# Feed-forward gate and up products by one level of Strassen's seven-product form

## The chip, the cores and the metric

The kernel runs on one core of one Trainium2 chip. The metric is the device time of one execution in microseconds (us), the median of three runs. Engines are named as in the profile: PE is TensorE (PEld its weight loads), DVE VectorE, ACT ScalarE, POOL GpSimd, SP SyncE, which issues most DMAs.

## The reference

One layer of a decoder on x of 512 x 1024: three token mixers, cross-attention, a SwiGLU feed-forward layer, each behind a residual and LayerNorm. What the change touches is the feed-forward layer, with D = 1024 and 2816 hidden features:

```
def swiglu(h, w_gu, w_down):
    gate, up = jnp.split(h @ w_gu, 2, axis=-1)
    return (jax.nn.silu(gate) * up) @ w_down
...
h = layer_norm(DN_ALPHA * h + swiglu(h, ffn_w_gu[l], ffn_w_down[l]), ln3_g[l], ln3_b[l])
```

## The kernel before

All of it stays in the core's memory except the weights, which stream in units of [128 x 1024] (512 KB). Matrix products run in fp32r, a reduced form, with operands split in two: a hi part (a copy into fp32r) and a lo part (the rest, again in fp32r). `mm3` makes three matmuls, hi by hi, hi by lo, lo by hi. For each weight unit ACT makes `whi` (copy of `raw`) and DVE `wlo` (`raw` minus `whi`). `take()` hands out a unit and at the same time issues the work for later ones: lo splits `AHEAD` = 3 units ahead, one hi split more, DMAs 3 further on; all these tiles come from one pool `wp` of 14 buffers of [128 x 1024].

The feed-forward layer has KF = 22 hidden tiles f of 128 features. `w_gu` holds two units for each f, gate then up; a unit is eight blocks of 128 input features (k) by 128 hidden features. `wstat` multiplies a unit by h2T, the transposed, split activations (eight k, 512 tokens, as two tiles c = 0, 1 of four k each): 24 matmuls of 512 columns into one PSUM bank, fg or fu. ACT makes Silu of fg (sl), DVE multiplies by fu, and sl is split again into act, the operand of the down projection `w_dn` (tiles p). The last eight splits wait until all f are done.

The first two f (four units) are special: h2T comes from the LayerNorm after cross-attention, tile by tile of 128 tokens (t = 0 to 3). For these units the first 256 columns (t = 0, 1) are multiplied before the tiles 2 and 3 are ready, and the second 256 columns behind them (PSUM tiles named f). A LayerNorm tile goes through ACT and DVE sums (lt, st), a power on POOL (st with mh), two DVE operations that make lh, and `ln_T`: per c four transposes into one PSUM bank (tp), an ACT copy h2Th and a DVE subtraction h2Tl, both from that bank.

Everything is recorded in the order in which the program is written: each engine runs its instructions in that order and waits for semaphores of the others. The generators of the LayerNorm tiles are run at `slot()` calls, by a cost model at build time. Every recorded operation stands on line 74 of before and line 75 of the changed kernel, so rows are told apart by their tile names.

Of the kernel before, what the change touches and what calls it, by code (L numbers as in the profile page):

```python
# [16 lines left out]
P = 128  # L17
# [140 lines left out]
def hybrid_kernel(ctx: ExitStack, tc: tile.TileContext, I, out, dbg=None):  # L158
# [25 lines left out]
    def W(s, dt):  # L184
        return wp.tile([P, 1024], dt, tag="w", name=nm(s))
# [52 lines left out]
    order += [("w_xv", i, 1024) for i in range(4, 8)]  # L238
    add("w_xq", 8)
    add("w_xo", 8)  # L240
    add("w_gu", 2 * KF)
    add("w_dn", KF)
    raws, splits = {}, {}
    st = {"dma": 0, "hi": 0, "split": 0}

    def dma_to(n):
        while st["dma"] < min(n, len(order)):
            i = st["dma"]
            name, j, size = order[i]
# [26 lines left out]
    def split_to(n):  # L276
        while st["split"] < min(n, len(order)):
            i = st["split"]
            hi_to(i + 1)
            st["split"] += 1  # L280
            if i < NK32:
                continue
            size = order[i][2]
            hi, lo, raw, whole = his.pop(i)
            if lo is None:
                low = W("wlo", F32R)
                lo = low[:, :size]
                splits[i] = (whole, low)
# [93 lines left out]

    def mm3(ps, w, x, first, last):
        T.matmul(ps, lhsT=w[0], rhs=x[0], start=first, stop=False)
        T.matmul(ps, lhsT=w[0], rhs=x[1], start=False, stop=False)
        T.matmul(ps, lhsT=w[1], rhs=x[0], start=False, stop=last)

    def cut(pair, *idx):
        return pair[0][idx], pair[1][idx]
# [967 lines left out]
    def proj_ln(name, actT, nk, hres, lnj, outT, final=False, need=None):  # L1357

        nu = nk // 2
        last = min(4, nu)

        def part(pss, un, w, ts, stop):
            for kk in range(2):
                k = 2 * un + kk
                for t in ts:
                    mm3(pss[t], cut(actT[k], ALL, slice(t * P, (t + 1) * P)),
                        cut(w, ALL, slice(kk * 512, kk * 512 + 512)), k == 0, stop and k == nk - 1)

        sts = [S("st", 7) for _ in range(NT)]

        def half(t, c, ps):
            V.scalar_tensor_tensor(hres[t][c], hres[t][c], ALPHA, ps, ALU.mult, ALU.add,
                                   accum_out=sts[t][:, c:c + 1])
            if c == 0:
                ln_first(hres[t][0], sts[t])

        first = [PS("p0") for _ in range(NT)]
        for un in range(nu):  # L1380
            w = take(name)
            if need is not None:
                need(un)
            part(first, un, w, range(NT), True)
            if un == 0:
                gb = ln_params(lnj)
            slot()
        second = [PS("p1") for _ in range(NT)]
        done = 0
        for un in range(nu - last):  # L1390
            w = take(name)
            part(second, un, w, range(NT), False)
            if done < NT:
                half(done, 0, first[done])
                done += 1
            slot()
        while done < NT:
            half(done, 0, first[done])
            done += 1
        ws = [take(name, min(AHEAD, NPAIR - 1 - un)) for un in range(last)]  # L1400
        hout, es = [None] * NT, []

        def tile_gen(t):
            h = ln_apply(hres[t], sts[t], gb)
# [6 lines left out]
            ln_T(h, t, outT)  # L1411
# [12 lines left out]
        return hout, es  # L1424
# [73 lines left out]
            slot()  # L1498
        eh.append(start_bg(head(h, qh)))

    def need_head(un):
        finish(eh[un])


    h2T8, h2T = new_T("h2T")
    h2, es = proj_ln("w_xo", oT, KD, h1, 2, h2T8, need=need_head)
    finish_all(es[0], es[1])
    pre = []
    for i in range(4):
        w = take("w_gu", min(AHEAD, NPAIR - 1 - i))  # L1510
        ps = PS("f0")
        wstat(ps, w, h2T, cols=slice(0, 256))
        pre.append((w, ps))
        slot()
    finish_all(*es)
    for i, (w, ps) in enumerate(pre):
        wstat(ps, w, h2T, cols=slice(256, 512))
        split_to(nxt[0] + AHEAD)
# [11 lines left out]

    act = [None] * KF
    late = []
    for f in range(KF):
        if pre:
            ps, ps2 = pre.pop(0), pre.pop(0)
        else:
            w = take("w_gu")
            ps = PS("fg")
            wstat(ps, w, h2T)
            ps2 = None  # L1540
        s = H("sl")
# [12 lines left out]
    del h2T
    for i, (f, s) in enumerate(late):
        if i % 4 == 0:
            l8 = (H8("act"), H8("act"))
        act[f] = (l8[0][:, i % 4], l8[1][:, i % 4])
        split(act[f][0], act[f][1], s)
# [95 lines left out]
```

## Time and profile before

| | |
|---|---|
| time, median of 3 runs | 1004.05 us (1003.15 to 1004.45) |
| profiled execution, its own time | 1004.38 us |
| its span, first to last instruction | 1002.7 us |
| PE busy | 985.8 us, 98% |
| DVE, ACT, POOL busy | 53%, 37%, 18% |
| mean granted clock of PE | 0.996 |

A busy share is an average over the whole span. What a stage waits for is read in that stage, from the chain that ended last and from the idle time ahead of single instructions. The granted clock is a share of 2.4 GHz.

### The profile page before, as it was taken

To read this page: it belongs to the slowest core of one execution; us is meant where nothing else is said; L and a number is where in the kernel's file an instruction comes from. 1 tells how busy PE (TensorE), PEld (TensorE's weight loads), DVE (VectorE), ACT (ScalarE), POOL (GpSimd) and SP (SyncE) were. 2 spreads that over 40 slices of the span, in tenths; PEclk is the share of its full clock that TensorE was granted. 3 is DMA by queue.
4 is the path that set the end of the run, shared out by engine and by line. 5 is a ranking of instruction groups with operands and counts; after the bars stand their busy time and mean duration, and the time that the engine had idled before them with its cause. 6 is when DMAs were issued, how large, how long until landed. Compare 5 with 4: busy or idle time off the path is not lost. (4 is left out here: it accounts for less than half of the span.)

```text
span 1002.7 us, 12403 instructions
## 1 busy us (share of the span) xinstructions
PE 985.8 (98%) x4856; PEld 816.1 (81%) x4856; DVE 532.8 (53%) x869; ACT 368.7 (37%) x598; POOL 185.3 (18%) x281
## 2 busy tenths in 40 slices
PE   9999999999999999999989999999999999999996
PEld 7788778877888888888878888988888888888885
DVE  5724897696586644465864547633423322342317
ACT  5644465523244225533354433332232222321301
POOL 1389960042515001020100000200000000000001
PEclk9999999999999999999999999999999999999999
DMA  9932223234343544354222311543342322222202
GB/s 348 346 128 88 83 99 116 86 104 128 105 137 129 166 148 143 135 199 165 89 102 83 105 64 42 180 167 111 126 131 84 105 106 84 106 105 106 84 21 85
DMA packets 38363, 123.75 MB, mean 123 GB/s; under 512 B 4864, under 2 KB 5280, under 8 KB 38304
## 3 DMA queue, kind: packets, MB, share of 16 engines
q1 hardware_dynamic: 29856, 97.79, 27.8%
q0 software_dynamic: 6592, 22.02, 6.7%
q10 hardware_dynamic: 1856, 3.15, 1.1%
q8 instruction: 38, 0.62, 0.2%
q14 instruction: 21, 0.17, 0.0%
HBM read 109.31 MB, written 11.53 MB: 121 GB/s over the span
## 5 line engine op out<-in xcount | busy, mean ns | idle before, releaser
L74 DVE TENSOR_TENSOR wlo<-raw,whi 128x1024 fp32r<-128x1024 f32 x162 | 196.8, 1233 | 84.8 <-PE p L74 52.1
L74 ACT ACTIVATE whi<-raw 128x1024 fp32r<-128x1024 f32 x162 | 169.4, 1057 | 99.0 <-PE p L74 45.0
L74 PE MATMUL p<-whi,act 128*128 128x512 f32 x352 | 108.4, 389 | 0.0
L74 DVE TENSOR_TENSOR sl<-sl,fu 128x512 f32<-128x512 f32 x20 | 13.8, 688 | 140.0 <-PE fu L74 92.5
L74 POOL TENSOR_TENSOR st<-st,mh 128x1 f32<-128x1 f32 x16 | 15.3, 957 | 393.7 <-DVE st L74 388.0
L74 PE MATMUL gt<-h0Th,whi 128*128 128x512 f32 x192 | 79.2, 413 | 0.0
L74 PEld LDWEIGHTS p<-whi,act 128*128 128x128 f32 x352 | 66.1, 188 | 13.7
L74 PE MATMUL gt<-h0Th,wlo 128*128 128x512 f32 x192 | 75.0, 391 | 0.0
L74 PE MATMUL gt<-h0Tl,whi 128*128 128x512 f32 x192 | 74.9, 390 | 0.0
L74 PE MATMUL p<-wlo,act 128*128 128x512 f32 x176 | 68.5, 389 | 0.0
L74 PE MATMUL fg<-h2Th,whi 128*128 128x512 f32 x160 | 62.3, 389 | 0.0
L74 PE MATMUL fg<-h2Tl,whi 128*128 128x512 f32 x160 | 62.3, 389 | 0.0
L74 PE MATMUL fg<-h2Th,wlo 128*128 128x512 f32 x160 | 62.2, 389 | 0.0
L74 PE MATMUL fu<-h2Th,whi 128*128 128x512 f32 x160 | 62.2, 389 | 0.0
L74 PE MATMUL fu<-h2Tl,whi 128*128 128x512 f32 x160 | 62.2, 389 | 0.0
L74 PE MATMUL fu<-h2Th,wlo 128*128 128x512 f32 x160 | 62.2, 389 | 0.0
L74 ACT ACTIVATE th<-gt,gbh 128x512 f32<-128x512 f32 x24 | 16.6, 692 | 99.2 <-PE gt L74 90.2
L74 ACT ACTIVATE sl<-fg 128x512 f32<-128x512 f32 x20 | 12.0, 598 | 97.7 <-PE fg L74 97.7
L74 PEld LDWEIGHTS gt<-h0Th,wlo 128*128 128x128 f32 x192 | 36.0, 188 | 7.7
L74 PEld LDWEIGHTS gt<-h0Th,whi 128*128 128x128 f32 x192 | 36.2, 189 | 5.8 <-issue 0.2
L74 PEld LDWEIGHTS gt<-h0Tl,whi 128*128 128x128 f32 x192 | 36.3, 189 | 5.6
L74 PE MATMUL p<-whi,oT 128*128 128x512 f32 x128 | 40.5, 391 | 0.0
(348 smaller groups left out, 2156.1 us busy)
## 6 DMA issues: line engine op xcount, KB each, us to landing
raw<-in_w_gu SPq DMA_DIRECT2D x44, 512.0 KB, 3.2
raw<-in_w_dn SPq DMA_DIRECT2D x22, 512.0 KB, 3.2
raw<-in_w_xk SPq DMA_DIRECT2D x8, 512.0 KB, 6.7
raw<-in_w_gatea SPq DMA_DIRECT2D x8, 512.0 KB, 3.2
raw<-in_w_gateb SPq DMA_DIRECT2D x8, 512.0 KB, 3.2
raw<-in_w_gatec SPq DMA_DIRECT2D x8, 512.0 KB, 3.8
raw<-in_w_xv SPq DMA_DIRECT2D x8, 512.0 KB, 3.6
raw<-in_w_mix SPq DMA_DIRECT2D x8, 512.0 KB, 3.5
```

The costliest lines, as they stand in the source:

```text
L74: return f(*a, **k)
```

## The change

The first four f stay in the plain form (two in halves, two whole). The other 18 are taken in 9 groups of two. In a group the weights of a pair of f and the activations are cut in two each: gate and up blocks by the two halves of k (b0: gate, lower half; b1: up, lower; b2: up, upper; b3: gate, upper, each [128 x 1024], loaded as two pieces of 256 KB), tokens in two halves of 256. Instead of eight products of half size there are seven, each of 24 matmuls of 256 columns, in the order 11, 12, s2, s1, s3, s4, 22 (p0 to p6 below), with the weights b0, b3, t2, t1, b2-b1, b2, t4. Here t1 = b1-b0, t2 = b2-t1, t4 = b3-t2. POOL makes these four differences, in the order t1, t2, b2-b1 (in place), t4. Sums of activations s1 to s4 are made on POOL too, once, from plain copies of the transposed tiles that ACT makes out of the tp banks; they are split like other operands.

The products 11, s2, s3 and 22 are summed in one PSUM bank, wb, s1 and s4 in wc, 12 is alone in wa. Partial sums are read out while the bank goes on being used: ACT copies wb after 11 (m1) and after s2 (u2), and wc after s1 (m5); DVE adds wa to m1, wb to m5 after s3, wc to u2 after s4. The results are sg = Silu(m1) * u2 and sh = Silu(wb) * m5. From the third group on one split of act is made per group; the others are made while `w_dn` runs, six k ahead (`need_act`). A DMA is now issued only when `room()` finds buffers for it.

```
+NPLAIN = 4
...
+        if n == 2:
+            load(1)
+            load(2)
+            b["t1"], b["t2"] = W("t1", F32), W("t2", F32)
+            G.tensor_tensor(b["t1"], b[1], b[0], ALU.subtract)
+            G.tensor_tensor(b["t2"], b[2], b["t1"], ALU.subtract)
+            del b[0]
+            return b["t2"]
+        if n == 3:
+            return b.pop("t1")
+        if n == 4:
+            G.tensor_tensor(b[1], b[2], b[1], ALU.subtract)
+            return b.pop(1)
+        if n == 5:
+            return b.pop(2)
+        t = W("t4", F32)
+        G.tensor_tensor(t, b[3], b["t2"], ALU.subtract)
...
-        dma_to(min(st["split"], i + 1 + AHEAD) + DMA_AHEAD)
+        prefetch(min(st["split"], i + 1 + AHEAD) + DMA_AHEAD)
...
+    def h2_T(h, t):
+        plain[t] = [H("hT0"), H("hT1")]
+        for c in range(2):
+            ps = PS("tp")
+            for i in range(4):
+                T.transpose(ps[:, i * P:(i + 1) * P], h[c][:, i * P:(i + 1) * P], ident)
+            dst = (ALL, ALL, slice(t * P, (t + 1) * P))
+            split(h2T8[0][c][dst], h2T8[1][c][dst], ps.rearrange("p (k t) -> p k t", t=P))
+            A.activation(plain[t][c], ps, AF.Copy)
+        if t < 2:
+            return
+
+        (a11, a12), (a21, a22) = plain[t - 2], plain[t]
+        G.tensor_tensor(a22, a21, a22, ALU.add)
+        G.tensor_tensor(a21, a11, a21, ALU.subtract)
+        G.tensor_tensor(a11, a22, a11, ALU.subtract)
+        G.tensor_tensor(a12, a12, a11, ALU.subtract)
+        sums[t] = {"s1": a22, "s2": a11, "s3": a21, "s4": a12}
...
+    def product(ps, w, n, first):
+
+        for e in range(2):
+            for k in range(4):
+                c = e * 512 + k * P
+                mm3(ps[:, 256 * e:256 * e + 256], cut(w, ALL, slice(c, c + P)), (pl[n, 0][k], pl[n, 1][k]),
+                    first and e == 0 and k == 0, k == 3, skip_group_check=True)
...
+    for d in range((KF - NPLAIN) // 2):
+        pa, pb, pc_ = PS("wa"), PS("wb"), PS("wc")
+        m1, m5, u2, sg, sh = H("m1"), H("m5"), H("u2"), H("sg"), H("sh")
+        step(pb, "11", True)
+        A.activation(m1, pb, AF.Copy)
+        step(pa, "12", True)
+        V.tensor_tensor(m1, pa, m1, ALU.add)
+        A.activation(sg, m1, AF.Silu)
...
+        step(pb, "s2")
+        A.activation(u2, pb, AF.Copy)
+        step(pc_, "s1", True)
+        A.activation(m5, pc_, AF.Copy)
+        step(pb, "s3")
+        V.tensor_tensor(m5, pb, m5, ALU.add)
+        step(pc_, "s4")
+        V.tensor_tensor(u2, pc_, u2, ALU.add)
+        V.tensor_tensor(sg, sg, u2, ALU.mult)
+        step(pb, "22")
+        A.activation(sh, pb, AF.Silu)
+        V.tensor_tensor(sh, sh, m5, ALU.mult)
...
+        if len(late) > 9:
+            act_split()
...
-    hout, es = proj_ln("w_dn", act, KF, hres, 3, None, final=True)
+    hout, es = proj_ln("w_dn", act, KF, hres, 3, None, final=True, need=need_act)
```

POOL's queue around the LayerNorm tiles and the first group. In before, behind the power of tile 2 (st, mh) stand the power of tile 3 and the DMAs that store h2:

```order
L74 TENSOR_TENSOR st_4975<-st_4975,mh 128x1
L74 TENSOR_TENSOR st_4976<-st_4976,mh 128x1
L74 TENSOR_TENSOR st_4977<-st_4977,mh 128x1
L74 DMA h2d<-lh_5284 128x512
L74 DMA h2d<-lh_5286 128x512
```

In the changed kernel the same place (hT are the plain copies):

```order
L75 TENSOR_TENSOR st_4976<-st_4976,mh 128x1
L75 TENSOR_TENSOR hT_5477<-hT_5476,hT_5477 128x512
L75 TENSOR_TENSOR hT_5476<-hT_5336,hT_5476 128x512
L75 TENSOR_TENSOR hT_5336<-hT_5477,hT_5336 128x512
L75 TENSOR_TENSOR hT_5337<-hT_5337,hT_5336 128x512
L75 TENSOR_TENSOR st_4977<-st_4977,mh 128x1
```

The four sums of tiles 0 and 2 have come in ahead of the power of tile 3.

ACT's queue in the middle of the hidden tiles. In before (sl reads fg, act is the hi part of a split):

```order
L74 ACTIVATE whi_6003<-raw_5936 128x1024
L74 ACTIVATE sl_6032<-fg_6007 128x512
L74 ACTIVATE whi_6036<-raw_5969 128x1024
L74 ACTIVATE act_6066<-sl_6032 128x512
L74 ACTIVATE whi_6072<-raw_6005 128x1024
```

In the changed kernel a group (t_6546 is t2, t_6545 t1, t_6681 t4 of the fourth group; raw_6539 is b2-b1; m is m1, then m5):

```order
L75 ACTIVATE whi_6549<-t_6546 128x1024
L75 ACTIVATE whi_6579<-t_6545 128x1024
L75 ACTIVATE sh_6381<-wb_6375 128x512
L75 ACTIVATE act_6607<-sl_5764 128x512
L75 ACTIVATE whi_6622<-raw_6539 128x1024
L75 ACTIVATE m_6614<-wb_6612 128x512
L75 ACTIVATE whi_6651<-raw_6542 128x1024
L75 ACTIVATE sg_6617<-m_6614 128x512
L75 ACTIVATE whi_6683<-t_6681 128x1024
L75 ACTIVATE u_6616<-wb_6612 128x512
L75 ACTIVATE whi_6715<-raw_6685 128x1024
L75 ACTIVATE m_6615<-wc_6613 128x512
```

Between two readings of wb (m, then u) now stand sg, which needs m with wa added by DVE, and the whi of t4, which needs POOL.

DVE's queue at the same place. In before:

```order
L74 TENSOR_TENSOR sl_5756<-sl_5756,fu_5764 128x512
L74 TENSOR_TENSOR act_5791<-sl_5756,act_5790 128x512
L74 TENSOR_TENSOR wlo_5794<-raw_5727,whi_5760 128x1024
L74 TENSOR_TENSOR wlo_5827<-raw_5729,whi_5796 128x1024
L74 TENSOR_TENSOR sl_5825<-sl_5825,fu_5833 128x512
```

In the changed kernel, the same group as above for ACT:

```order
L75 TENSOR_TENSOR wlo_6537<-raw_6480,whi_6510 128x1024
L75 TENSOR_TENSOR u_6379<-wc_6376,u_6379 128x512
L75 TENSOR_TENSOR sg_6380<-sg_6380,u_6379 128x512
L75 TENSOR_TENSOR wlo_6577<-t_6546,whi_6549 128x1024
L75 TENSOR_TENSOR sh_6381<-sh_6381,m_6378 128x512
L75 TENSOR_TENSOR act_6608<-sl_5764,act_6607 128x512
L75 TENSOR_TENSOR wlo_6619<-t_6545,whi_6579 128x1024
L75 TENSOR_TENSOR wlo_6649<-raw_6539,whi_6622 128x1024
L75 TENSOR_TENSOR m_6614<-wa_6611,m_6614 128x512
L75 TENSOR_TENSOR wlo_6679<-raw_6542,whi_6651 128x1024
L75 TENSOR_TENSOR wlo_6713<-t_6681,whi_6683 128x1024
```

The addition of wa to m (m1) stands behind the wlo of t2, t1 and b2-b1, where before a multiplication came after two wlo.

## Rows read from the trace of the kernel before

**Rows 1.** The page: the span, and busy us (share) xinstructions of each engine.

```profile
span 1002.7 us, 12403 instructions
...
PE 985.8 (98%) x4856; PEld 816.1 (81%) x4856; DVE 532.8 (53%) x869; ACT 368.7 (37%) x598; POOL 185.3 (18%) x281
```

**Rows 2.** The chain that ended last: start us, us, engine, tile, xinstructions.

```profile
634.88 8.63 PE f L74 x72
643.51 0.45 PE tp L74 x4
...
645.36 11.66 PE f L74 x95
...
662.48 5.44 PE fu L74 x24
...
874.64 119.69 PE p L74 x528
```

**Rows 3.** Stretches: from:to us, busy of each engine, PEclk, DMA share, GB/s.

```profile
512.00:516.00 4.00, 3.19 (x9) 2.55 (x10) 4.00 (x8) 1.11 (x2) 0.00 (x0) 0.71 0.11 45
516.00:520.00 4.00, 4.00 (x16) 3.21 (x15) 0.89 (x1) 0.03 (x1) 0.00 (x0) 0.86 0.00 0
...
644.00:648.00 4.00, 3.41 (x27) 2.97 (x26) 1.29 (x2) 1.07 (x2) 0.00 (x0) 1.00 0.93 363
...
656.00:874.00 218.00, 218.00 (x967) 180.66 (x966) 68.26 (x73) 61.25 (x78) 4.92 (x9) 1.00 0.32 110
```

**Rows 4.** Timeline of POOL with DVE idle: start us, us, operation, sizes.

```profile
86.40 0.46 POOL L74 TENSOR_TENSOR pw<-pw 128x128 f32<-128x128 f32 x1
...
253.03 1.08 POOL L74 TENSOR_TENSOR phr<-pq,pq 128x512 f32<-128x512 f32 x1
...
255.21 1.28 POOL L74 TENSOR_TENSOR phr<-phr,pht 128x512 f32<-128x512 f32 x1
256.45 1.07 POOL L74 TENSOR_TENSOR phi<-pq,pq 128x512 f32<-128x512 f32 x1
```

**Rows 5.** Groups by form: xcount | busy us, mean ns | idle before, releasers.

```profile
L74 DVE TENSOR_TENSOR wlo<-raw,whi 128x1024 fp32r<-128x1024 f32 x162 | 196.8, 1233 | 84.8 <-PE p L74 52.1 <-ACT whi L74 26.1 <-issue 2.9
L74 DVE TENSOR_TENSOR sl<-sl,fu 128x512 f32<-128x512 f32 x20 | 13.8, 688 | 140.0 <-PE fu L74 92.5 <-issue 39.6 <-ACT act L74 7.9
...
L74 ACT ACTIVATE whi<-raw 128x1024 fp32r<-128x1024 f32 x162 | 169.4, 1057 | 99.0 <-PE p L74 45.0 <-DVE wlo L74 15.1 <-issue 12.5
L74 ACT ACTIVATE sl<-fg 128x512 f32<-128x512 f32 x20 | 12.0, 598 | 97.7 <-PE fg L74 97.7
```

**Rows 6.** Timeline of DVE and POOL, 130 to 134 us.

```profile
130.09 1.51 POOL L74 TENSOR_TENSOR pht<-pq,pq 128x512 f32<-128x512 f32 x1
130.60 2.09 DVE L74 TENSOR_TENSOR wlo<-raw,whi 128x1024 fp32r<-128x1024 f32 x1
131.68 2.16 POOL L74 TENSOR_TENSOR phr<-phr,pht 128x512 f32<-128x512 f32 x1
```

**Rows 7.** Timeline of DVE and POOL at 317 us; br is a PSUM tile.

```profile
317.18 1.29 POOL L74 TENSOR_TENSOR phr<-phr,pht 128x512 f32<-128x512 f32 x1
...
317.56 0.69 DVE L74 SCALAR_TENSOR_TENSOR th<-th,br 128x512 f32<-128x512 f32 x1 [3.53 <-PE br L74]
```

**Rows 8.** DMA issues: xcount, KB each, median us from issue to landing.

```profile
raw<-in_w_gu SPq DMA_DIRECT2D x44, 512.0 KB, 3.2
...
res<-h2d POOLq DMA_DIRECT2D x8, 256.0 KB, 3.0
```

**Rows 9.** Timeline of ACT, POOL and DVE in the LayerNorm tiles, 634 to 641 us.

```profile
634.48 1.08 ACT L74 ACTIVATE h2Th<-tp 128x512 fp32r<-128x512 f32 x2 [0.94 <-PE tp L74]
...
638.23 0.99 POOL L74 TENSOR_TENSOR st<-st,mh 128x1 f32<-128x1 f32 x1 [10.49 <-DVE st L74]
...
639.25 1.42 DVE L74 SCALAR_TENSOR_TENSOR lh<-lt,st,lnp 128x512 f32<-128x512 f32 x2 [0.44 <-POOL st L74]
```

**Rows 10.** Timeline of PE at 512 us, with the idle time before.

```profile
512.81 0.50 PE L74 MATMUL xq<-h1Tl,whi 128*128 128x512 f32 x1 [2.77 <-DVE h1Tl L74]
```

More of the change, by code (lines that the diff above doesn't have):

```diff
@@ L240, in hybrid_kernel @@
     add("w_xo", 8)
-    add("w_gu", 2 * KF)
+    add("w_gu", 2 * NPLAIN)
+    for d in range((KF - NPLAIN) // 2):
+        for n in range(7):
+            order.append(("w_gu", (NPLAIN + 2 * d, n), 1024))
     add("w_dn", KF)
     raws, splits = {}, {}
+    blk = {}
     st = {"dma": 0, "hi": 0, "split": 0}
@@ L285, in split_to @@
             if lo is None:
-                low = W("wlo", F32R)
-                lo = low[:, :size]
-                splits[i] = (whole, low)
+                lo = W("wlo", F32R)[:, :size]
+                splits[i] = (whole, lo)
             else:
@@ L293, in hybrid_kernel, with room, prefetch @@
     nxt = [0]
+    keep = [0]
+    def room():
+        names = {x.name for b in blk.values() for x in b.values()} | {x.name for x in raws.values()}
+        names |= {x[2].name for x in his.values()}
+        return 2 * max(keep[0], 1) + 2 * len(splits) + len(his) + len(names) + 2 <= NBUF_W
+    def prefetch(n):
+        while st["dma"] < min(n, len(order)) and (not keep[0] and type(order[st["dma"]][1]) is int or room()):
+            dma_to(st["dma"] + 1)
     def take(name, ahead=AHEAD):
@@ L380, in finish_all, with mm3 @@
                     rush[0] = False
[L383 to L386, printed above, removed]
+    def mm3(ps, w, x, first, last, **k):
+        T.matmul(ps, lhsT=w[0], rhs=x[0], start=first, stop=False, **k)
+        T.matmul(ps, lhsT=w[0], rhs=x[1], start=False, stop=False, **k)
+        T.matmul(ps, lhsT=w[1], rhs=x[0], start=False, stop=last, **k)
     def cut(pair, *idx):
@@ L1410, in tile_gen @@
             yield T, h[0], h[1]
-            ln_T(h, t, outT)
+            if callable(outT):
+                outT(h, t)
+            else:
+                ln_T(h, t, outT)
             yield 0
@@ L1499, in hybrid_kernel, with need_head @@
         eh.append(start_bg(head(h, qh)))
-    def need_head(un):
-        finish(eh[un])
+    def need_head(k):
+        finish(eh[k // 2])
     h2T8, h2T = new_T("h2T")
-    h2, es = proj_ln("w_xo", oT, KD, h1, 2, h2T8, need=need_head)
+    pl, wr = {}, {}
+    for n, c, half in (("11", 0, 0), ("12", 1, 0), ("21", 0, 1), ("22", 1, 1)):
+        for part in range(2):
+            wr[n, part] = [h2T8[part][c][:, :, 256 * half:256 * half + 256]]
+            pl[n, part] = [h2T8[part][c][:, k, 256 * half:256 * half + 256] for k in range(4)]
@@ new lines, in place, with to_block @@
+    def place(n, part, *tiles):
+        m = 4 // len(tiles)
+        pl[n, part] = [tiles[j // m][:, (j % m) * 256:(j % m) * 256 + 256] for j in range(4)]
+        wr[n, part] = [x[:, 0:256 * m].rearrange("p (k t) -> p k t", t=256) for x in tiles]
+    def to_block(n, t, src):
+        ts = slice((t % 2) * P, (t % 2) * P + P)
+        src = src.rearrange("p (k t) -> p k t", t=P)
+        hi, lo = wr[n, 0], wr[n, 1]
+        m = max(len(hi), len(lo))
+        for i in range(m):
+            ks = slice(4 // m * i, 4 // m * (i + 1))
+            at = [x[i][:, :, ts] if len(x) == m else x[0][:, ks, ts] for x in (hi, lo)]
+            split(at[0], at[1], src[:, ks])
@@ new lines, in hybrid_kernel @@
+    plain, sums = {}, {}
+    def h2_T(h, t):
[15 more added lines that the diff above has]
+        sums[t] = {"s1": a22, "s2": a11, "s3": a21, "s4": a12}
@@ L1515, in hybrid_kernel @@
     finish_all(*es)
-    for i, (w, ps) in enumerate(pre):
-        wstat(ps, w, h2T, cols=slice(256, 512))
-        split_to(nxt[0] + AHEAD)
+    del h1T, kx, vx, oT, h1
+    place("s1", 0, big.tile([P, 1032], F32R, tag="gx", name=nm("s1"), bufs=1))
+    place("s1", 1, big.tile([P, 1024], F32R, tag="tz", name=nm("s1")))
+    place("s2", 0, big.tile([P, 1024], F32R, tag="tz", name=nm("s2")))
+    place("s2", 1, H("s2", F32R), H("s2", F32R))
+    for part in range(2):
+        place("s4", part, H("s4", F32R), H("s4", F32R))
+    for i, (w, ps) in enumerate(pre):
+        half_plain(ps, w, 1)
+        if i < 3:
+            for t in (2, 3):
+                n = ("s2", "s1", "s4")[i]
+                to_block(n, t, sums[t][n])
+        keep[0] -= 1
+        split_to(nxt[0] + min(AHEAD, i + 1))
+        prefetch(st["split"] + DMA_AHEAD)
     pre = [ps for w, ps in pre]
@@ L1554, in hybrid_kernel, with act_tiles, act_split @@
[L1554 to L1559, printed above, removed]
+    l8 = []
+    def act_tiles(fs, t2s, s):
+        late.append((fs, t2s, s))
+    def act_split():
+        fs, t2s, s = late.pop(0)
+        n = len(t2s)
+        if len(late) < 8:
+            if not l8 or l8[0][2] == 4:
+                l8[:] = [[H8("act"), H8("act"), 0]]
+            hi, lo = l8[0][0][:, l8[0][2]], l8[0][1][:, l8[0][2]]
+            l8[0][2] += 1
+        else:
+            hi, lo = H("act", F32R), H("act", F32R)
+        split(hi, lo, s)
+        for i, f in enumerate(fs):
+            act[f] = act[f] or [None] * NT
+            for j, t in enumerate(t2s):
+                o = slice((i * n + j) * P, (i * n + j + 1) * P)
+                act[f][t] = (hi[:, o], lo[:, o])
@@ new lines, in hybrid_kernel, with place_s3 @@
+    for f in range(NPLAIN):
+        s = H("sl")
+        for i in range(2):
+            if f > 1:
+                w = take("w_gu")
+                pre.append(PS("fg" if i == 0 else "fu"))
+                wstat(pre[-1], w, h2T)
+                slot()
+            if i == 0:
+                A.activation(s, pre[0], AF.Silu)
+        V.tensor_tensor(s, s, pre[1], ALU.mult)
+        del pre[:2]
+        act_tiles([f], range(NT), s)
+    def place_s3():
+        for part in range(2):
+            pl["s3", part], wr["s3", part] = pl["21", part], wr["21", part]
+        for t in (2, 3):
+            to_block("s3", t, sums[t]["s3"])
+        sums.clear()
+        plain.clear()
@@ new lines, in product, with step @@
+    def product(ps, w, n, first):
+        for e in range(2):
+            for k in range(4):
+                c = e * 512 + k * P
+                mm3(ps[:, 256 * e:256 * e + 256], cut(w, ALL, slice(c, c + P)), (pl[n, 0][k], pl[n, 1][k]),
+                    first and e == 0 and k == 0, k == 3, skip_group_check=True)
+    def step(ps, n, first=False):
+        product(ps, take("w_gu"), n, first)
+        slot()
+    for d in range((KF - NPLAIN) // 2):
+        pa, pb, pc_ = PS("wa"), PS("wb"), PS("wc")
[5 more added lines that the diff above has]
+        A.activation(sg, m1, AF.Silu)
+        if d == 0:
+            place_s3()
+        step(pb, "s2")
[10 more added lines that the diff above has]
+        V.tensor_tensor(sh, sh, m5, ALU.mult)
+        fs = [NPLAIN + 2 * d, NPLAIN + 2 * d + 1]
+        act_tiles(fs, (0, 1), sg)
+        act_tiles(fs, (2, 3), sh)
+        if len(late) > 9:
+            act_split()
+        del m1, m5, u2, sg, sh, pa, pb, pc_
@@ L1560, in hybrid_kernel, with need_act @@
+    pl.clear()
+    wr.clear()
+    def need_act(k):
+        while late and (act[min(k + 6, KF - 1)] is None or None in act[min(k + 6, KF - 1)]):
+            act_split()
     hres = load_res(h2d)
-    hout, es = proj_ln("w_dn", act, KF, hres, 3, None, final=True)
+    hout, es = proj_ln("w_dn", act, KF, hres, 3, None, final=True, need=need_act)
     finish_all(*es)
```

52 lines of the change are left out of this document (27 added, 25 removed).

## The prediction

> **What bounds the kernel now.** I read the page first: the span is 1002.7 us and TensorE (PE) is busy for 985.8 of it, the other engines for about half or less [rows 1]. Then the chain that ended last: behind the LayerNorm tiles it is nothing but PE, 24 matmuls per weight unit of the feed-forward layer, and then the down projection p without a break [rows 2]. The table by stretches says the same: from 656 to 874 us PE is busy 218.00 of 218.00 us at granted clock 1.00, VectorE (DVE) 68, ScalarE (ACT) 61, GpSimd (POOL) 5 [rows 3]. So less PE time shortens the kernel directly, and every wait that the change puts before a matmul lengthens it directly; there is no slack to hide one in.
>
> **Term 1, the products.** A 512-column matmul takes 119.69 us / 528 = 226.7 ns in p, and 5.44 / 24 = 226.7 in fu; a 256-column one, with its own weight load as here, 8.63 / 72 = 119.9 ns [rows 2]. Half the columns cost 0.53, not 0.5. Eighteen of 22 f leave the plain form: 36 units x 24 = 864 matmuls x 226.7 = 195.8 us. In their place come 9 groups x 7 products x 24 = 1512 matmuls x 119.9 = 181.3 us. Term 1 is **-14.5 us**; a group of two f goes from 21.8 to 20.15 us, a product is 2.88.
>
> **Term 2, GpSimd's sums, and what they hold up.** Each group needs t1, t2, b2-b1 and t4, subtractions of 128x1024 in SBUF, which no row shows. With two dense inputs 128x512 takes 1.28 us and 128x128 0.46 [rows 4]: 2.14 ns an element, so 1024 take about 2.38; as starts stand 0.04 before the end ahead of them, I take G = 2.3. Bounds: twice the 1.08 of the same size with operands that repeat, less one fixed part of 0.18, is 1.98; twice 1.28 is 2.57. The dense row is nearest.
>
> The Trainium skill, "GPSIMD Engine Reference", section 3.1, gives 4497 ns for a two-input addition of 2048 elements; half of it, 2.25, is an estimate by that page. By it the sum below comes out 1.4 us lower. The row stays.
>
> DVE and POOL don't run side by side here. At 130.09 a POOL operation is running; the wlo that DVE starts at 130.60 lasts 2.09 us, against 1.23 on the average [rows 5, 6], and the POOL operation behind it, 131.68, lasts 2.16, against 1.28. Each waits for the other to end. A DVE operation with one input in PSUM was not held: 0.69 us in the middle of a POOL one [rows 7]. So I treat each operation of two SBUF inputs as exclusive; m1, m5 and u2, added from PSUM, are not.
>
> The Trainium skill, "SBUF — State Buffer", section "Who interferes with whom", speaks against this change: a DVE instruction with two SBUF inputs and a GpSimd one that reads SBUF share one pair of ports, and the later waits for the whole of the earlier. By that rule the waits below must come, without it term 2 would be nil; the rows at 130 us agree with it.
>
> Now one group, in us from the start of its fifth product (p4, s3), in the order in which the engines are fed. Durations: wlo 1.15 and whi 1.0 in a row, a 512 operation 0.65 on DVE and 0.6 on ACT [rows 5].
> - The loads of the next group's b1 and b2 get buffers when p3 ends and land about 3.2 later [rows 8], SP having two more to issue: t1 can start at 3.5. It runs to 5.8; a wlo that waits meanwhile follows to 6.95; t2 to 9.25.
> - b2-b1 and the DVE multiplication sg*u2 share the next 2.3 + 0.65, whichever is first: 12.2. wlo of t2 to 13.35, sh*m5 and the lo of act to 14.65.
> - t4 needs the buffer of b3, free when the next group's second product (p1) ends at 14.4. It and the wlo of t1 take 3.45, again in either order: 18.1. wlo of b2-b1 to 19.25.
> - Only now does DVE come to m1 += wa, which could have run at 14.6: it ends at 19.9. ACT has Silu (sg) next and behind it, in its fixed order, the whi of t4 and then the copy u2 = wb: 20.5, 21.5, 22.1.
> - p4 of the next group writes over the bank that this copy reads. It was due at 20.15 and starts at 22.1: about 1.9 us a group. Some of that falls on p3, if t4 goes ahead of the wlo of t1; the sum is the same.
>
> The chain holds four POOL operations, so p4 starts at 12.9 + 4G: on time for G below 1.8. The first groups begin with idle queues; I charge seven of the nine: **+13.3 us**. Bounds of G: 0.7 a group (+4.7) and 3.0 (+21). Landings 0.5 later add 3.5. [...]
>
> **Term 3, the LayerNorm tiles.** Before, ACT has h2Th of tile t=2 done at 635.5, POOL the power of tile 3 at 638.23 to 639.2 and DVE its lh at 640.7, well ahead of PE, which transposes it at 643.51 when the first halves of four units are done [rows 2, 9]. Each plain copy added on ACT comes behind h2Tl of DVE, which reads the same bank and itself stands behind lh and wlo; ACT then makes its three whi later. For t=1 the two copies cost PE about 0.35 us (h2Th of c=1 comes after the first copy). For t=2 the copies and the later whi put the end of its second copy at about 639.8. POOL then makes the four sums of tiles 0 and 2 (4 x 1.28 = 5.1, and 0.7 for DVE between), and only behind them the power of t=3, its place in POOL's queue: 645.6 to 646.6. With the first lh 0.75 later (two take 1.42 [rows 9]) the transposes start at 647.4, where PE, 0.35 late, was ready at 643.9: 3.5 us idle. A last 0.5 is the copy between the two h2Th of t=3. Together 4.4.
>
> So long a pause lowers the clock. After 2.77 us of idle PE the granted clock was 0.71 and 0.86 in the next two stretches of 4 us [rows 3, 10], 1.2 GHz for part of them: (0.29 + 0.14) x 4 = 1.7 us lost. Term 3 is **+6.1 us**, from 2 (copies not in the way, sums ended within the slack of 2.8) to 9 (DVE's chain of small operations held by each sum as well).
>
> **At nothing.** Further loads: twice as many pieces of half the size, 256 KB landing in 3.0 us, 512 KB in 3.2 [rows 8]; SP only issues. The splits of s1, s2, s3, s4 lie under the second halves of four units, 11.66 us [rows 2], and under the plain f of 21.8, on engines that are a third busy; if they came late, the third product would wait for them, once. The splits of act that w_dn now asks for as it goes lie under p of 2.7 us a k, against 1.3 for one split. In the down projection nothing else changes.
>
> **Sum.** -14.5 + 13.3 + 6.1 = +4.9 us: span 1007.6. Outside the span lie 1.7 us (the profiled execution has 1004.38), which makes 1009.3; the profiled execution stands 0.3 above the median of the runs, so the median should be **1009.0**. What a measurement can tell from no change is 0.2%, 2.0 us: faster is below 1002.0, slower above 1006.1.
>
> **Rivals.** First, faster: the sums fit under the products. One mechanism decides, the length of a POOL subtraction. At G = 2.1 the wait is 1.2 a group, 8.4 in seven, and the gain and both losses cancel; at 1.98 the time is 1000.4; and if POOL and DVE were not exclusive for these operands, term 2 is nil and the time 994 to 996. For it: the 1.08 row, and that POOL is otherwise idle. Against: both operands are dense, and rows 6. Chance 0.28.
>
> Second, longer waits: G = 2.57, or landings of 3.7, since loads now wait for buffers that only POOL frees: 1013 to 1020. For it: the 2.16 row, and that POOL is never the one that goes first in my chain. Against: loads land in 3.2 with DMA a third busy. Chance 0.17.
>
> Third, the change doesn't do what it says: a 256-column matmul in a group runs longer than 119.9, because the weight loads show 816.1 us of busy time [rows 1] and there are as many as matmuls. 10% more would be 18 us: 1027. Against it stands the row of 72 such matmuls with as many loads. Chance 0.03.
>
> **How the numbers follow.** The forecast has 0.52, its own range is 1005 to 1014 (G from 2.15 to 2.45, term 3 from 4 to 8). Of the 0.28 of the first rival 0.04 lies above 1002.0, and that part and 0.08 of the forecast's lower end are within 0.2%: same 0.12. Faster holds the other 0.24 of the first rival, and 0.02 from a forecast whose term 3 vanishes: 0.26. Slower is the rest, 0.42 + 0.17 + 0.03 = 0.62. The range that leaves out 0.1 on each side reaches into both rivals: 997 to 1018.
>
> **What would show it.** In the trace after: matmuls of the products 120 ns apart; POOL's 128x1024 subtractions 2.2 to 2.4 us where alone, 3 and more where DVE is ahead; wlo up to 3.4; PE idle before the first matmul of s3 by ACT's u2 (or before s1 by DVE's wlo of t1), 1.5 to 2.3 us from the third group on; the period of a group 21.5 to 22.5; PE idle before tp of t=3 by 3 to 5 us, with the clock below 1.00 behind it. If the groups come every 20.2 us, term 2 was wrong; if tp comes at 644, term 3.

## The result, and the profile after

The changed kernel takes **1019.94 us** (median of 4 runs, 1018.62 to 1021.16) beside 1004.25 for the kernel before (median of 4 in the same runs): ratio 1.0154, 95% interval 1.0134 to 1.0175. It is slower, as forecast, but by 15.7 us where 4.9 were forecast, and it lies 1.9 us above the range (997 to 1018).

The page, for [rows 1] and [rows 8]:

```profile
span 1019.5 us, 14088 instructions
...
PE 981.0 (96%) x5504; PEld 840.3 (82%) x5504; DVE 633.9 (62%) x935; ACT 417.1 (41%) x672; POOL 288.9 (28%) x325
...
raw<-in_w_gu SPq DMA_DIRECT2D x72, 256.0 KB, 3.9
```

PE does less work (981.0 us for 985.8), and the span is 16.8 longer. The chain that ended last, for [rows 2]:

```profile
652.94 12.71 PE f L75 x95
665.65 5.47 PE fg L75 x24
...
687.43 2.87 PE wb L75 x24
690.31 2.88 PE wa L75 x24
...
891.59 114.28 PE p L75 x504
```

The stages are cut in the timeline of PE, at the first matmul of f, of fg, of what the groups replace (of the groups themselves in the changed kernel) and of p. Before:

```profile
630.23 0.28 PE L74 MATMUL f<-h2Th,whi 128*128 128x256 f32 x1
656.85 0.40 PE L74 MATMUL fg<-h2Th,whi 128*128 128x512 f32 x1
678.64 0.39 PE L74 MATMUL fg<-h2Th,whi 128*128 128x512 f32 x1
874.48 0.39 PE L74 MATMUL p<-whi,act 128*128 128x512 f32 x1
```

and after:

```profile
631.59 0.28 PE L75 MATMUL f<-h2Th,whi 128*128 128x256 f32 x1
665.48 0.40 PE L75 MATMUL fg<-h2Th,whi 128*128 128x512 f32 x1
687.27 0.28 PE L75 MATMUL wb<-h2Th,whi 128*128 128x256 f32 x1
891.43 0.40 PE L75 MATMUL p<-whi,act 128*128 128x512 f32 x1
```

This cuts the difference in three. The first matmul of f comes 1.4 us later. That isn't due to the change: its first new operation, ACT's plain copy of tile 0, stands at 624.81 us, and 1.3 of the 1.4 are there at 599.92 already (598.61 before). Behind the pause at 512 us the granted clock was 0.50 and 0.65 in the two stretches of [rows 3], for 0.71 and 0.86 before. In the runs below this matmul stands anywhere from 629.81 (e1) to 632.20 (e12). From it to the first fg PE needs 33.9 us, before 26.6: **+7.3**. The nine groups take 204.2 us, for 195.8 of the plain form: **+8.3**, where -1.2 was forecast. From p to the end it is 128.1 us, for 128.2. The products run at the forecast pace (2.88 us for 24), so the groups hold some 24 us beyond what they need without a wait (180.3 us, e1 below). The timeline of PE, for a group, the last group and tile 3 of the LayerNorm (in brackets idle us and what ended it):

```profile
650.44 1.94 PE L75 MATMUL tp<-ident,lh 128*128 128x128 f32 x8 [4.11 <-DVE lh L75]
...
786.39 0.38 PE L75 MATMUL wb<-h2Th,whi 128*128 128x256 f32 x1 [0.98 <-ACT u L75]
802.01 0.50 PE L75 MATMUL wb<-s,whi 128*128 128x256 f32 x2 [0.96 <-ACT m L75]
805.53 0.39 PE L75 MATMUL wc<-s,wlo 128*128 128x256 f32 x1 [0.18 <-DVE wlo L75]
809.36 0.38 PE L75 MATMUL wb<-h2Th,whi 128*128 128x256 f32 x1 [0.93 <-ACT u L75]
...
877.31 0.38 PE L75 MATMUL wb<-h2Th,whi 128*128 128x256 f32 x1 [0.99 <-ACT u L75]
884.13 0.80 PE L75 MATMUL wc<-s,whi 128*128 128x256 f32 x2 [3.69 <-ACT m L75]
```

The waits are largely where the forecast has them: 0.9 to 1.1 us before s3 by the copy u2, in eight groups, and 0.2 before s1 by DVE's wlo in six. Those before s2, 0.3 to 1.0 us by the copy m1, it doesn't name. From the first s3 that waits, 719.78, to the last, 877.31, seven groups take 22.50 us each. The last group has a pause of its own, 3.69 us before s4, by the copy m5, which nothing in the forecast pays for. The chain through one group says why 22.50:

```profile
807.21 1.14 DVE wlo L75
...
808.75 0.43 SPq L75
...
810.94 4.85 DMA raw<-in_w_gu
...
817.11 2.73 POOL t L75
...
819.87 1.07 ACT whi L75
...
820.96 1.47 DVE wlo L75
...
823.20 0.68 DVE sh L75
...
824.41 4.56 DVE wlo L75 x2
828.97 0.60 DVE m L75
829.57 1.14 DVE wlo L75
```

It begins and ends with the same instruction, the wlo of b2, 22.36 us apart, and PE isn't in it. The wlo of b2-b1 frees the buffer for the next group's b0, for which SP has waited 14.5 us (806.64), and the wlo of b2 the one for b3, 0.8 us more; the loads of b1 and b2 stand behind these in SP's queue, so that all eight pieces go out from 806.64 to 810.94. They land, POOL makes t1 and t2, ACT and DVE split t2, DVE is held by t4 (two wlo in 4.56 us), adds wa to m1, and only then comes to the next wlo of b2. What POOL and DVE do there, from the timeline:

```profile
814.62 2.40 POOL L75 TENSOR_TENSOR t<-raw,raw 128x1024 f32<-128x1024 f32 x1 [10.83 <-DVE wlo L75]
817.11 2.73 POOL L75 TENSOR_TENSOR t<-raw,t 128x1024 f32<-128x1024 f32 x1
819.79 2.40 POOL L75 TENSOR_TENSOR raw<-raw,raw 128x1024 f32<-128x1024 f32 x1
824.15 2.60 POOL L75 TENSOR_TENSOR t<-raw,t 128x1024 f32<-128x1024 f32 x1 [1.96 <-issue]
...
824.41 3.42 DVE L75 TENSOR_TENSOR wlo<-t,whi 128x1024 fp32r<-128x1024 f32 x1
```

t1 starts 5.3 us after s3 (809.36), not 3.5; alone, a subtraction takes 2.40; and the wlo of t1 lasts 3.42, because t4 began 0.26 us ahead of it.

### The profile page after: what moved, and what is told of

The parts are those of the page before. It is cut to its first block, busy times and chain, and to the rows that moved or that the text cites. A ratio compares the mean times of both kernels' runs of the same rounds, so it can differ in the third digit from the quotient of the medians.

```text
span 1019.5 us, 14088 instructions
## 1 busy us (share of the span) xinstructions
PE 981.0 (96%) x5504; PEld 840.3 (82%) x5504; DVE 633.9 (62%) x935; ACT 417.1 (41%) x672; POOL 288.9 (28%) x325
## 5 line engine op out<-in xcount | busy, mean ns | idle before, releaser
L75 DVE TENSOR_TENSOR wlo<-t,whi 128x1024 fp32r<-128x1024 f32 x27 | 52.2, 1934 | 31.8 <-ACT whi L75 31.8
L75 PE MATMUL wb<-h2Th,whi 128*128 128x256 f32 x216 | 61.9, 287 | 7.9 <-ACT u L75 7.9
L75 PE MATMUL wb<-h2Tl,whi 128*128 128x256 f32 x216 | 61.1, 283 | 0.0
L75 PE MATMUL wb<-h2Th,wlo 128*128 128x256 f32 x216 | 61.1, 283 | 0.0
L75 PE MATMUL wc<-s,whi 128*128 128x256 f32 x288 | 53.9, 287 | 3.7 <-ACT m L75 3.7
L75 POOL TENSOR_TENSOR t<-raw,t 128x1024 f32<-128x1024 f32 x18 | 49.8, 2766 | 21.4 <-issue 14.5
L75 ACT ACTIVATE whi<-t 128x1024 fp32r<-128x1024 f32 x27 | 27.6, 1049 | 63.8 <-POOL t L75 63.8
L75 PEld LDWEIGHTS wb<-h2Th,whi 128*128 128x128 f32 x216 | 41.4, 191 | 9.5 <-ACT u L75 9.5
L75 PEld LDWEIGHTS wc<-s,whi 128*128 128x128 f32 x288 | 45.6, 195 | 3.9 <-ACT m L75 3.9
L75 POOL TENSOR_TENSOR t<-raw,raw 128x1024 f32<-128x1024 f32 x9 | 21.6, 2403 | 91.9 <-DMA raw<-in_w_gu 39.2
L75 PE MATMUL wc<-s,wlo 128*128 128x256 f32 x144 | 41.7, 289 | 1.2 <-DVE wlo L75 1.2
```

The lines of the kernel that those rows point to most:

```text
L75: return f(*a, **k)
```

## The experiments

All are compared with the kernel before in the same runs. The stages are read from the timeline of PE of one execution each, as above: f to fg, and the nine groups from their first matmul to the first of p. The same operations differ a little from run to run: the f stage, the same program in e3, e4 and the change, takes 33.9, 33.4 and 33.9 us, and the period of a group (from s3 to the next s3) is 22.50 us in the change and 22.78 in e4, whose groups but the last are the same program too.

| run | median us | ratio, 95% interval | f stage | groups |
|---|---|---|---|---|
| before | 1004.25 | | 26.6 | 195.8 (plain) |
| the change | 1019.94 | 1.0154, 1.0134 to 1.0175 | 33.9 | 204.2 |
| e1 no weight sums | 996.44 | 0.9918, 0.9901 to 0.9935 | 33.2 | 180.3 |
| e2 activation sums late | 1018.37 | 1.0139, 1.0119 to 1.0159 | 29.5 | 207.1 |
| e3 u2 ahead of sg | 1022.88 | 1.0175, 1.0157 to 1.0192 | 33.9 | 207.8 |
| e4 whi of w_dn behind m5 | 1019.23 | 1.0140, 1.0123 to 1.0156 | 33.4 | 204.9 |
| e5 weight sums on DVE | 1009.07 | 1.0038, 1.0023 to 1.0053 | 34.0 | 193.7 |
| e6 15 buffers | 998.28 | 0.9932, 0.9916 to 0.9949 | 33.3 | 182.5 |
| e7 no t4 | 1000.06 | 0.9951, 0.9936 to 0.9965 | 33.3 | 183.8 |
| e8 e2, copies behind both splits | 1015.42 | 1.0103, 1.0088 to 1.0118 | 26.6 | 206.1 |
| e9 e8 and 15 buffers | 990.70 | 0.9853, 0.9839 to 0.9868 | 26.6 | 182.1 |
| e10 before, 15 buffers | 1005.63 | 1.0000, 0.9990 to 1.0009 | 26.6 | 195.8 (plain) |
| e11 e5 and 15 buffers | 1010.41 | 1.0050, 1.0030 to 1.0069 | 33.3 | 193.0 |
| e12 b1, b2 loaded by POOL | 1030.53 | 1.0245, 1.0225 to 1.0266 | 33.2 | 210.4 |
| e13 b1, b2 loaded ahead of b3 | 1004.59 | 0.9992, 0.9979 to 1.0005 | 33.3 | 189.6 |

**e1, without the weight sums.**

```
-            G.tensor_tensor(b["t1"], b[1], b[0], ALU.subtract)
-            G.tensor_tensor(b["t2"], b[2], b["t1"], ALU.subtract)
...
-            return b["t2"]
+            return b[2]
...
-            return b.pop("t1")
+            return b[1]
...
-            G.tensor_tensor(b[1], b[2], b[1], ALU.subtract)
...
-        G.tensor_tensor(t, b[3], b["t2"], ALU.subtract)
+        t = b[3]
```

> Leaves out the four weight sums of each group on POOL: the products take the loaded blocks themselves, with the same loads, splits, products and readouts. Theory (POOL's sums, exclusive with DVE's operations, set the period of a group): the period falls from 22.5 us to 20.2 to 20.5, about 17 us less in eight groups, so about 1003; the wait before the last group's s4 stays. Rival (the loads are late, landing 4 to 6 us after issue, and the sums only ride behind them): ACT's whi then wait for the loads in place of the sums, the period stays above 21.8, and the time is 1013 or more.

The groups take 180.3 us, 20.03 each, and PE waits nowhere in them, not in the last one either; the wait there, which the theory kept, is gone too, and the time is 996.44 for its 1003. So the products are worth what term 1 says (181.3), all of the waiting comes with the sums, and the loads alone, in the same order, are in time. It doesn't say which of the sums' effects it is: without them the buffers are free earlier too.

**e2, the activation sums behind all four tiles.**

```
-        if t < 2:
-            return
...
+    def h2_sums(t):
...
     finish_all(*es)
+    for t in (2, 3):
+        h2_sums(t)
```

> The activation sums on POOL are recorded behind all four LayerNorm tiles, not ahead of the power of tile 3. Theory (POOL's queue order delays tile 3): the transposes of tile 3 start some 5 us earlier, PE's pause there falls below 2 us and the granted clock stays at 1.00, so 4.5 to 6 us less, about 1014.5. Rival (the plain copies and DVE's chain behind them are the delay): tile 3 still comes late, under 2 us less, about 1018.5.

The f stage is 4.4 us shorter, PE's pauses before tile 3 are 0.66 and 0.96 us and the clock stays at 1.00 there: POOL's queue was the larger part of its loss. The time fell by less, since the groups took 3.0 us more (period 22.96 between the same places). In e4 seven periods are 2 us longer than in the change as well, with the same program; what the rest comes from is not shown. The 1.6 us between the medians prove neither number of the expectation; the stages do.

**e3, the copy u2 ahead of Silu.**

```
-        A.activation(sg, m1, AF.Silu)
...
         A.activation(u2, pb, AF.Copy)
+        A.activation(sg, m1, AF.Silu)
```

> Silu (sg) is recorded behind the copy u2, so that this copy no longer stands behind m1 += wa and the Silu on ACT. Theory A (only ACT's order makes PE wait at s3): the wait of about 1.2 us before s3 goes in eight groups, about 10 us less, 1010. Theory B (the pair POOL and DVE is nearly full, 19.6 of 20.15 us a group, and what is saved at s3 comes back as waits before s2 and s1): 2 to 5 us less, 1015 to 1018.

Neither: 1022.88 us, not less than the change (the two intervals overlap, so the 3 us more prove nothing either). PE doesn't wait before s3 any more, but before s4 and s2. From ACT's timeline of this run, ahead of the copy m5:

```profile
765.88 1.06 ACT L75 ACTIVATE whi<-raw 128x1024 fp32r<-128x1024 f32 x1 [2.26 <-DMA raw<-in_w_gu]
766.85 0.58 ACT L75 ACTIVATE m<-wc 128x512 f32<-128x512 f32 x1
```

ACT stands 2.26 us for a load. The wait on PE has moved to the next instruction that needs something of the loop. PE is idle in the groups for 17.4 us in all, about as in the change (16.7). What makes them 3.6 longer is the clock: the pauses are fewer and longer, and behind three of them, of 1.72, 2.62 and 2.16 us, the granted clock fell, with 1.7 us lost each time. For the first (PEclk is the last figure but two, as in [rows 3]; (0.33 + 0.10) x 4 us):

```profile
780.00:784.00 4.00, 3.04 (x16) 3.04 (x17) 4.00 (x3) 1.85 (x3) 2.12 (x1) 0.67 0.01 2
784.00:788.00 4.00, 4.00 (x32) 4.00 (x32) 4.00 (x5) 2.24 (x3) 0.00 (x0) 0.90 0.33 96
```

In the change it stays at 1.00 in the groups until the last one.

**e4, the last group.**

```
+        if d == (KF - NPLAIN) // 2 - 1:
+            cap[0] = nxt[0] + 4
         step(pc_, "s1", True)
         A.activation(m5, pc_, AF.Copy)
+        cap[0] = 99999
```

(`take` splits no unit beyond `cap`.)

> In the last group the whi of the first w_dn unit is recorded behind the copy m5 and not ahead of it. Theory (ACT's order: m5 waits behind a whi whose load lands late): PE's pause of 3.7 us before s4 goes, with what the clock lost behind it, 4 to 5.6 us less, about 1015. Rival (the load of w_dn itself is late, whatever the order): PE waits as long for wlo of w_dn before the first p, within 1 us of 1020.

The rival was nearer. The pause before s4 is gone; PE waits 2.47 us before 22 instead, since m5 += wb now stands behind a wlo of w_dn on DVE:

```profile
884.86 1.23 DVE L75 TENSOR_TENSOR wlo<-raw,whi 128x1024 fp32r<-128x1024 f32 x1 [5.87 <-ACT whi L75]
886.00 0.68 DVE L75 TENSOR_TENSOR m<-wb,m 128x512 f32<-128x512 f32 x1
```

The load of w_dn is late; every queue that asks for it ahead of the readouts passes this on. In the runs whose groups aren't held (e1, e6, e9) the same order costs nothing.

**e5 and e11, the weight sums on DVE**, with 14 and with 15 buffers: `G.` becomes `V.` in the four subtractions.

> All else as in the change, but the four weight sums of a group are made by DVE, not POOL, at the same places. Theory (two-input POOL operations of 2.4 us that exclude DVE are what the groups wait for): DVE has 4 x 1.15 = 4.6 us more of its own but is never held; 17.9 of 20.15 us a group are busy, the period falls below 21, and the time to 1003 to 1008. Rival (any serial sum behind late loads delays the splits; DVE, in fixed order, now also waits for the loads itself): the period stays at 22 to 23 or grows, 1016 to 1025.

> Fifteen weight buffers and the four weight sums of a group on DVE. Theory (what set the period was a loop closed by the loads; without it either engine's sums fit under the products): groups of 20.1 to 20.4 us, 997 to 1001. Rival (with the sums DVE's own queue is the bound, loads or not): 1005 to 1010.

Without the exclusion 10.5 us of the 24 go, but 13 stay (period 21.6 from the second s3 to the last, between what e5's theory and its rival had), and another buffer doesn't help (193.7 and 193.0 us). In e11 PE waits 0.4 to 1.3 us before one of the products into wb in seven of the nine groups, released by DVE's m. That DVE's own queue is the bound, as e11's rival had it, is shown in part only: the time, 1010.41, is just above the rival's range, but DVE is busy for only 83.0 of 107.9 us in five groups, it waits 11.3 us there for loads, and the chain that ended last still comes back to a load in each group (781.65, 803.23, 824.34 us). With the loads in time POOL is the better place for the sums (e6, next).

**e6 and e10, fifteen buffers**, in the change and in the kernel before (`NBUF_W = 15`, `NHEAP = 50`).

> Fifteen weight buffers instead of fourteen (and 50 tiles in the heap instead of 52); POOL's sums as in the change. Theory (sums and exclusion alone): the period stays at 22.3 to 23, within 2 us of the change. Rival (the landing of b1 and b2, whose buffers come free late, is part of the cycle that repeats): t1 starts less than 4 us after s3 instead of 5.2 to 5.9, the period falls by 1 us or more, 8 us or more less in all.

> The kernel before with fifteen weight buffers and a heap of 50. Theory (PE waits for nothing in its feed-forward layer, so a buffer more gives nothing): 1003.5 to 1005.5. Rival (the buffer alone, not the products, made the fifteen-buffer run faster): 997 to 1000.

The rival of e6 is right, beyond its number: the groups take 182.5 us, 20.3 each, with every sum and all the exclusion in place. The kernel before gains nothing. What SP waited for between 719 and 872 us (us in total, times, longest), in the change:

```profile
SPq L75 <- DVE wlo L75: 91.8, 13, 14.5
SPq L75 <- DMA raw<-in_w_gu: 24.9, 14, 2.7
```

and with fifteen buffers:

```profile
SPq L75 <- DVE wlo L75: 67.2, 19, 5.6
SPq L75 <- PE wa L75: 60.6, 7, 9.6
```

In the change SP waited for a wlo ahead of b0 and again ahead of b3; now it waits last for a product (12, in wa) ahead of b0 and for a wlo ahead of b1, and the longest wait for a wlo falls from 14.5 to 5.6. So the eight loads of a group no longer go out together but in two bursts of four (from 792.48 and from 798.39 us, say), and the second half of b1 lands 3.3 us after its issue, in the change 4.9 (medians of the nine groups). POOL of that run (a group whose s3 starts at 839.95, and the t4 ahead of it):

```profile
835.06 3.18 POOL L75 TENSOR_TENSOR t<-raw,t 128x1024 f32<-128x1024 f32 x1 [3.64 <-issue]
842.93 2.41 POOL L75 TENSOR_TENSOR t<-raw,raw 128x1024 f32<-128x1024 f32 x1 [4.69 <-DMA raw<-in_w_gu]
845.41 3.26 POOL L75 TENSOR_TENSOR t<-raw,t 128x1024 f32<-128x1024 f32 x1
```

t1 starts 3.0 us after s3, and now it is t2 and t4 that are held (3.26, 3.18): the exclusion is still there and falls on POOL, which has the time (busy for 57.7 of 102.0 us in five groups).

**e7, without t4** (`t = b[3]` in place of the last subtraction; the product 22 takes b3).

> Leaves out one of the four weight sums, t4 (the product 22 takes b3 itself). Theory (the operations of POOL and DVE stand one behind the other in a chain, 2.4 us each): the whole of the wait of 2.35 us a group is gone, period 20.2 to 20.6, about 17 to 20 us less than the change, near 1001. Rival (it is the first two sums, t1 and t2 behind the late loads, that matter): the period stays above 21.5, 1012 or more.

183.8 us, 20.4 a group. A loop of 22.4 that loses one of its held pieces (t4 is 2.6 us of POOL and 2.3 of waiting on DVE) comes to about the 20.03 of PE; PE pauses for 1.6 us in all. But without t4 a buffer is free as well, as in e6, so this run doesn't show which of the two did it.

**e8, copies behind both splits of a tile**, with e2.

```
             split(h2T8[0][c][dst], h2T8[1][c][dst], ps.rearrange("p (k t) -> p k t", t=P))
-            A.activation(plain[t][c], ps, AF.Copy)
+            tps.append(ps)
+        for c in range(2):
+            A.activation(plain[t][c], tps[c], AF.Copy)
```

> The activation sums behind all four LayerNorm tiles, as in the run before, and both plain copies of a tile behind both of its splits, so that h2Th of c=1 no longer waits behind a copy that waits for DVE. Theory: PE's pause of 1.5 us before the first h2Tl matmuls of c=1 and the one of 0.7 to 1 us before tile 3 shrink to 0.5 or less; the f stage ends 1.5 to 3 us earlier than with the late sums alone, if the groups keep their period. Rival: DVE's own order (lh and wlo ahead of h2Tl) holds them as before, no change.

The f stage is back at 26.6 us, that of before: all of term 3 was the place of the copies in ACT's queue and of the sums in POOL's.

**e9, both mended.**

> Fifteen weight buffers, the activation sums behind all LayerNorm tiles, and the copies of a tile behind both of its splits. Theory (two separate losses, the closed loop of loads and sums in the groups and the order in the LayerNorm tiles): both gains add, groups of 20.1 us and an f stage that ends as in the kernel before, 989 to 992. Rival (they are one: earlier tiles only let the groups run into late sums or loads): 995 to 998.

The gains add: 990.7 us, 1.5% faster than before (ratio 0.9853). Of the 14.7 us the chain shows 13.8 at p, which starts at 860.86 instead of 874.64 [rows 2]:

```profile
857.98 2.88 PE wb L75 x24
860.86 114.28 PE p L75 x504
```

**e12, the loads of b1 and b2 issued by POOL.**

```
-                SP.dma_start(b[k][:, 512 * e:512 * e + 512], ...
+                (G if k in (1, 2) else SP).dma_start(b[k][:, 512 * e:512 * e + 512], ...
```

> Fourteen buffers as in the change; the loads of b1 and b2 are issued by POOL, ahead of t1, no longer by SP behind the load of b3, which waits for the wlo of b2. They now wait only for the end of the product s1. Theory (SP's order closes the loop: wlo of b2, load of b3, loads of b1 and b2, t1, and so on to the next wlo of b2): t1 starts 4 to 4.7 us after s3 instead of 5.2 to 5.9, the period falls from 22.5 to 21 to 21.8 us, the time to 1008 to 1015. Rival (the chain from s3 on, sums and exclusion, is the bound; POOL's issuing of four DMAs, 0.55 us each, only comes on top): period 22.5 or more, 1019 to 1030.

Inconclusive for the loop: t1 came no earlier. From the timeline of POOL, in a group whose s3 starts at 790.50:

```profile
789.96 2.18 POOL L75 DMA_DIRECT2D raw<-in_w_gu  x4 [5.03 <-ACT whi L75]
796.24 2.39 POOL L75 TENSOR_TENSOR t<-raw,raw 128x1024 f32<-128x1024 f32 x1 [4.10 <-DVE wlo L75]
```

That is 5.7 us after s3. The loads didn't start much earlier than by SP: 0.54 us ahead of s3 in this group, in the change 0.14, as they waited for ACT's whi here. And they still went out in a burst with SP's: they land after 4.9 us (median), SP's other four after 3.3. That isn't POOL's queue as such, since the same four, issued last by SP in the change, took 4.8.

**e13, the same question on SP**: fourteen buffers, only the order of the loads changed.

```
         if n == 1:
+            load(1)
+            load(2)
             load(3)
             return b[3]
         if n == 2:
-            load(1)
-            load(2)
```

> Fourteen buffers, all operations as in the change; SP issues a group's loads of b1 and b2 ahead of that of b3 (with the order the buffers of these tiles, and so the waits on them, change hands). Theory (the loop runs through the loads of b1 and b2, queued on SP behind one that waits for the wlo of b2): t1 starts 2.5 to 4 us after s3 instead of 5.2 to 5.9, the period falls below 21.2, the time to 1000 to 1008. Rival (the sums and the exclusion from s3 on are the bound with fourteen buffers, whenever the loads come): period above 22, 1016 or more.

15 us less than the change with the same number of buffers and the same operations; the groups take 189.6. The theory has the time right, not the period (below 21.2); the rival is out. PE doesn't wait until the fourth group; from then on s3 stands at 760.22, 781.95, 803.48, 825.20, 846.14 and 868.02, periods of 21.6 us, and t1 starts between 3.1 and 4.5 us after it. So the time at which b1 and b2 are loaded does set the period with fourteen buffers. With the order, the buffers that tiles take over change too (b1 itself now waits for a wlo), and b1 stands earlier in the burst; so SP's order, the buffers behind it and the crowding aren't told apart.

## Why the prediction was wrong, by its steps

**Right.** PE bounds the kernel, and a wait costs at least its length. Term 1 (-14.5): the groups of e1 take 180.3 us for 181.3. The price of a POOL subtraction, 2.38 from the dense row: 2.40 alone (2.3 was taken). That POOL and DVE exclude each other, both ways: t2 2.73, wlo of t1 3.42. The Trainium skill's rule, "SBUF — State Buffer", section "Who interferes with whom", that the later of the two waits for the whole of the earlier, fits these rows too. The place of the wait, in the main: s3 by ACT's u2 from the second group on, s1 by a wlo from the fourth.

**The step that failed** is the first of the group's list in term 2, "The loads of the next group's b1 and b2 get buffers when p3 ends and land about 3.2 later [rows 8], SP having two more to issue: t1 can start at 3.5". What SP had to issue first were loads that wait for DVE: b0 for the wlo of b2-b1, b3 for the wlo of b2, which stand at the end of the forecast's own list, before and behind m1 += wa. So the list isn't a chain that begins anew at each s3; it is a loop, and its end is its beginning. And as these waits end 1.7 us apart, eight pieces of 256 KB go out in one burst: the first lands after 2.6 us, those of b1 after 4.1 and 4.9, the last after 5.3 (medians of the nine groups), where 3.2 was taken for all. t1 started 4.9 to 6.0 us after the s3 that waits, not 3.5, and the period was 22.50, 2.47 over the 20.03 of PE, where 1.9 was charged. With the 1.1 of the group before these seven that is 18.4 us, for 13.3. More telling than the size is that the formula 12.9 + 4G names only the sums: one buffer (e6) took away 21.7 us with all four sums in place, and another order of the loads (e13) 14.6. How much of it is the late issue and how much the crowded landing, no run separates.

Term 2 also puts nothing for the clock behind its waits. In the change this holds up to the last group (1.00, with pauses of 1.1 us at most); in e3 it doesn't (5.1 us lost behind three pauses).

**Priced at nothing, and wrong:** the passage to the down projection. ACT's whi of the first w_dn unit, recorded ahead of the copy m5, waited for a load that landed 7.87 us after the wlo that let it go; s4 paused for 3.69 us and then ran in 4.58 instead of 2.88 at a lowered clock; the last group lost 5.5 us by it. The stretches (PEclk is the last but two):

```profile
652.00:656.00 4.00, 3.85 (x19) 3.35 (x18) 1.68 (x3) 2.46 (x6) 0.56 (x1) 0.58 0.00 0
...
880.00:884.00 4.00, 0.44 (x4) 0.24 (x2) 0.38 (x1) 1.47 (x2) 0.55 (x1) 1.00 1.03 413
884.00:888.00 4.00, 3.87 (x20) 3.88 (x21) 2.67 (x3) 1.69 (x3) 0.00 (x0) 0.57 1.02 397
```

At 880 us the DMA engines are full (share 1.03): loads of w_dn and the eight of res, which POOL issues as soon as its last sum is done, come together. No run was made to tell the crowding from the late issue, but other traces speak for the crowding: in e6 the first load of w_dn, issued 3.9 us ahead of the res loads, landed after 3.6 us and the third, in their midst, after 8.8; in e1, where the res loads are spread from 787 to 827 us, the first took 3.8.

**Mis-sized:** term 3, 7.3 us for 6.1. The pause before the transposes of tile 3 was 4.11 us for 3.5, the clock behind it 0.58 in one stretch, 1.2 GHz for most of it, and the wait of c=1 at t=1 grew from 0.47 us before to 1.55, where 0.35 more was charged (the h2Tl stands behind the copy). The mechanism, POOL's and ACT's order, is shown by e2 and e8: 4.4 and 2.9 us.

Then the sum: -15.5 (term 1, 180.3 for 195.8) + 18.4 + 5.5 + 7.3, and 1.4 that lies ahead of the change, is 17.1; the stretch from p to the end is 0.2 shorter, which leaves 16.9, for 16.8 in the span.

**The rivals.** "The sums fit under the products" was given to the length of a POOL subtraction, with G below 2.1. They do fit, with G at 2.4, when the loads are in time (e6). The second rival, "landings of 3.7, since loads now wait for buffers", had the cause in part, and its 1013 to 1020 holds the measured 1019.94; that is in part luck, since 5.5 us of it come from the passage to the down projection, G wasn't 2.57, and t1 came 1.4 to 2.5 us late, not 0.5: it added the later landing once to a chain.

## What to carry to other kernels

Where a change lengthens the time for which buffers are held, follow each new wait on a buffer through its queue to the work that frees it: if that work depends on what the queue loads, the two form a loop, and its length, not the length of any operation in it, is the period. Here a buffer more (21.7 us in the groups) or another order of the loads (14.6) was worth more than sums of half the length on another engine (e5, 10.5). On engines in fixed order an instruction that waits for a load belongs behind the readouts of running banks, and one-off sums behind the small operations for which the next tile waits.

## What was not expected of the hardware

A load of 256 KB took 3.9 us (median) in the groups, longer than 512 KB before (3.2). Where it stands in the burst of eight decides: 2.6 us for the first, 5.3 for the last (medians). A two-input subtraction of 128x1024 takes POOL 2.40 us, twice the 1.22 of DVE (e5), and still POOL was the better place (e6 and e11, 12 us apart), with the exclusion falling on the engine that has time to spare. A pause of PE isn't followed by a lower clock each time: behind one of 1.72 us (e3, 780.96) it was 0.67, behind one of 2.42 us (e12, 830.38) it stayed at 1.00.
